# w_xo of a hybrid encoder layer as a block product of seven products, with its sums made in DRAM

## Chip, cores and metric

One core of a Trainium2 chip runs the whole layer. The metric is the time of one execution on the device in microseconds (us), the median of three runs; lower is better. The engines are TensorE (PE: matmuls; PEld: loads of the stationary operand), VectorE (DVE), ScalarE (ACT), GpSimd (POOL) and SyncE (SP, which here only issues DMAs).

## The reference

An encoder layer on x of 512 tokens by 1024 channels, all in float32: two mixers that are merged by gates, then cross-attention to a memory of 256 tokens with four heads of 256, then a SwiGLU feed-forward part of width 2816, then a final norm. The part that is changed is the end of the cross-attention:

```
q = (hn @ w_q).reshape(bsz, seq, XATTN_HEADS, XATTN_HEAD_DIM)
...
p = jax.nn.softmax(s, axis=-1).astype(v.dtype)
o = jnp.einsum('bhlm,bmhd->blhd', p, v).reshape(bsz, seq, D_MODEL)
return o @ w_o
...
h = h + memory_cross_attention(rms_norm(h, xattn_norm_g[i]), memn,
                               w_q[i], w_k[i], w_v[i], w_xo[i])
h = h + swiglu(rms_norm(h, ffn_norm_g[i]), w_gate[i], w_up[i], w_down[i])
return rms_norm(h, final_norm_g)
```

`w_o` is the kernel's `w_xo`, 1024 by 1024.

## The kernel before

**Products in two parts.** Each float32 operand is split into a high part, rounded to the format of the matmul (`hi`, a ScalarE cast), and the rest (`lo`, a VectorE subtraction): `split`, lines 83 to 86. A product is three matmuls, hi·hi, hi·lo and lo·hi (`mm3`). The sum of squares of a norm runs on ScalarE, the power -1/2 on GpSimd, the scaling on VectorE, and TensorE transposes the result to channels by tokens (`norm_feat`, `to_feat`).

**The plan of weights.** `plan` lists every weight block in the order of its use, with the function that loads it and the one that splits it. `next_w` (line 330) hands out entry i; it also issues the loads of the entries some places ahead (`LOADS` = 3, for the feed-forward jobs 4 to 7) and the splits of the next two. Raw blocks, hi and lo have three buffers each. Most blocks are 512 KB, 128 partitions by 1024.

**Block products of seven.** The weights of `w_proj_b`, `w_q`, the feed-forward jobs (`plan_unit`) and `w_down` are multiplied in blocks of two by two with seven products instead of eight (Strassen's scheme with fewer additions, numbered 1 to 7). That needs sums of weight blocks: 4, 5, 6 and 7 are made of blocks of the matrix, 1, 2 and 3 are plain blocks. For `w_proj_b`, `w_q` and `w_down` DMAs make these sums ahead in a scratch tensor in DRAM: a copy on SP's queue and an accumulating DMA on GpSimd's queue. `plan_sums` (line 257) says at which entries of the plan each pair is issued, and pins the copies in the order of the program. In a feed-forward job the sum is made in SBUF (tile `t`). The left operand needs sums of token blocks in the same way; results are added onto each other in PSUM or by VectorE.

**The order of the work.** The program gives the order of priorities and a scheduler orders each engine's instructions by its own estimate of time. `in_order` keeps an instruction at its place; `later(n, f)` puts work off by n steps; `tick` counts steps.

**Around the change.** After the products of `w_q` come, for the four heads, `scores` (softmax over 256 memory tokens; VectorE and ScalarE), `turn` (transposes of the probabilities, split into p_hi and p_lo) and `values` (line 1399: the product with V into bank `po`, split into ot_hi and ot_lo). The output product `w_xo` is a plain one: for the left 512 columns `tokm` (line 1475) with four token blocks of 128, eight row blocks of 128 and three matmuls each; its hooks `second` and `last_two` put the values of heads 1 to 3 between. The right 512 columns come next, token blocks 0 and 1, then 2 and 3 (lines 1486 to 1500). `add_evac` (line 1291) adds a result to the residual h and sums squares; `feat_norm` makes fn, the normed input of the feed-forward part, for one token block at a time. The feed-forward part starts with `gate_part(0, T0)` (line 1575) on tokens 0 to 255 and the first 512 rows, T1 are tokens 256 to 511. `idle_product` (line 1114) is one matmul whose result nobody reads, pinned at its place in TensorE's order.

PSUM has five banks of the pool `bank` and three of `aux`. The pools of the feed-forward part open where those of the attention close (`at.close()`).

Of the kernel before, what the change touches and what calls it, by code (L numbers as in the profile page):

```python
# [9 lines left out]
F32 = mybir.dt.float32  # L10
F32R = mybir.dt.float32r
# [41 lines left out]
def hybrid_layer_kernel(  # L53
# [173 lines left out]

    def plan_units(units, down):
# [25 lines left out]
    def down_sum(q, c):  # L254
        return dsum[q][:, 2 * c:min(2 * c + 2, NF // 2), :]

    def plan_sums(places):
# [10 lines left out]
        for q, i, jc, more in ((5, 0, 0, lambda c: down_block(0, 1, c)), (7, 0, 1, lambda c: down_block(1, 1, c)),  # L268
                               (6, 1, 1, lambda c: down_sum(5, c)), (4, 1, 0, lambda c: down_sum(6, c))):
            for c in range(CHUNKS):  # L270
                jobs.append((down_sum(q, c), down_block(i, jc, c), more(c)))
# [44 lines left out]
    plan_tok(w_xo, 0, KD)  # L316
    for i in range(4):
        plan_block(w_xo, 2 * i, 2, 512, 512, place=(None, None, 2, 4)[i])
# [1080 lines left out]
    def values(hd, p_hi, p_lo):  # L1399
        for dt_ in range(2):  # L1400
# [4 lines left out]
            split(ot_hi[:, 2 * hd + dt_, :], ot_lo[:, 2 * hd + dt_, :], ps)  # L1405
# [49 lines left out]
    ot_lo = slot("E", (P, KD, T), F32R, "ot_lo")  # L1455
    values(0, *pts.pop(0))
    probs2 = scores(2)
    probs3 = scores(3)
    turn(1, probs1)
# [10 lines left out]
    g_f = gain(ffn_norm_g[0], "g_f")  # L1470
    ot = (ot_hi, ot_lo)
    fn_hi, fn_lo = token_slot("fn", AWAY)
    fn = (fn_hi, fn_lo)

    tokm(w_xo, 0, ot, KD, add_evac(0, 1, None), hooks={1: second, 2: last_two})
# [6 lines left out]
    full = fp.tile([P, KD, T], F32, tag="full", name="full", bufs=1)  # L1482


    fin = add_evac(1, 1, feat_norm(g_f, fn_hi, fn_lo, full))
    held = []
    for t0 in (0, 2):
        ps = {t: bank(f"pt{t - t0}") for t in (t0, t0 + 1)}
        for wi in range(2):
            if t0 == 0:  # L1490
                held.append((wi,) + next_w(w_xo, 2 * wi, 2, 512, 512))
            for t in ps:
                tok_block(ps[t], t, held[wi:wi + 1], ot, 2, slice(0, 512), wi == 0, False)
            tick(2.7)
        if t0 == 0:
            held += [(wi,) + next_w(w_xo, 2 * wi, 2, 512, 512) for wi in (2, 3)]
        for t in ps:
            tok_block(ps[t], t, held[2:4], ot, 2, slice(0, 512), False, True)
            fin(t, ps[t])
            tick(2.7)  # L1500
# [133 lines left out]
    for i, u in enumerate(UNITS):  # L1634
# [7 lines left out]
        if i == 0:  # L1642
            split(*fn_q(K0, T1), s3)
# [165 lines left out]
```

## Time and profile before

| | |
|---|---|
| median of three runs | 892.96 us (892.39 to 893.35) |
| the profiled execution's own time | 893.12 us |
| its span, first to last instruction | 891.3 us |
| mean granted TensorE clock | 0.997 |
| TensorE busy | 881.1 us, 5744 matmuls |
| VectorE busy | 642.5 us |
| ScalarE busy | 487.4 us |
| GpSimd busy | 106.9 us |
| moved by DMA | 165.36 MB |

A page of the profile shows busy times, the span in 40 slices, DMA queues, the chain of work that ended last, and the costliest groups of instructions. L86 is line 86 of the kernel. `out<-in` names the tiles an instruction writes and reads; `pt` are the banks of w_xo, `po` those of the values. A listed matmul is longer than the distance to the next one, since matmuls overlap. In a list of waits stand the engine, what it waited to do, for whom, the sum, the times and the longest.

### The profile page before, as it was taken

What the parts mean: (1) busy time and instruction counts of PE and PEld (TensorE: products, weight loads), DVE (VectorE), ACT (ScalarE), POOL (GpSimd) and SP (SyncE); (2) the same over time, 40 slices, a digit from 0 to 9 for tenths busy, and PEclk for the clock granted to TensorE, in tenths of its full rate; (3) what the DMA queues carried; (4) which work ended last, traced back from release to release, by engine and by line L of the source; (5) the groups of instructions that cost most, each with busy time, mean ns of one, the idle gap of its engine ahead of it and who ended that gap; (6) DMA issues with size and microseconds to landing.
All of it is one profiled execution on the core that took longest, in us unless ns stands there. A gap on an engine that the chain in (4) does not pass through costs nothing.

```text
span 891.3 us, 14796 instructions
## 1 busy us (share of the span) xinstructions
PE 881.1 (99%) x5744; PEld 788.0 (88%) x5744; DVE 642.5 (72%) x1048; ACT 487.4 (55%) x714; POOL 106.9 (12%) x165
## 2 busy tenths in 40 slices
PE   9999999999999999999999999999999999999996
PEld 6788888888889998889899978999999999988875
DVE  5697653889847368658856836676878777899875
ACT  5743994244396254347656534645555455655664
POOL 1005301111032111001001001101121111000010
PEclk9999999999999999999999999999999999999998
DMA  8667456978533789834579747627899999356672
GB/s 255 196 189 182 114 155 177 189 191 190 159 87 84 212 285 268 288 117 140 168 221 256 194 103 197 166 81 181 213 237 233 216 225 249 95 167 207 204 230 102
DMA packets 118408, 165.36 MB, mean 186 GB/s; under 512 B 11825, under 2 KB 84161, under 8 KB 118210
## 3 DMA queue, kind: packets, MB, share of 16 engines
q1 hardware_dynamic: 97474, 135.74, 47.9%
q0 software_dynamic: 20576, 28.15, 19.9%
q8 instruction: 45, 0.74, 0.3%
q10 hardware_dynamic: 288, 0.52, 0.2%
q14 instruction: 25, 0.20, 0.1%
HBM read 157.61 MB, written 46.63 MB: 229 GB/s over the span
## 4 chain that ended last, share of the span: by engine, by line
PE 97%; DMA 1%; SPq 1%; ACT 0%; DVE 0%; issue 0%; POOLq 0%; ACTq 0%
PE pf L358 26%; PE pt L358 17%; PE px L1110 12%; PE dx L358 6%; PE pq L1110 6%; PE dq L358 3%; PE pv L1110 3%; PE bx L1110 3%; PE qx L1110 2%; PE dv L358 2%; PE pz L871 2%; PE pk L814 2%; PE bq L1110 1%; PE qv L1110 1%; PE psc L358 1%; PE qq L1110 1%
## 5 line engine op out<-in xcount | busy, mean ns | idle before, releaser
L86 DVE TENSOR_TENSOR wlo<-wraw,whi 128x1024 fp32r<-128x1024 f32 (+1 forms) x145 | 172.2, 1189 | 101.2 <-ACT whi L85 101.0
L85 ACT CAST whi<-wraw 128x1024 fp32r<-128x1024 f32 (+1 forms) x145 | 148.6, 1026 | 152.2 <-PE pf L358 44.0
L358 PE MATMUL pf<-xn,whi 128*128 128x512 f32 x448 | 139.6, 391 | 0.0
L358 PEld LDWEIGHTS pf<-xn,whi 128*128 128x128 f32 x448 | 83.7, 188 | 17.0
L358 PE MATMUL pf<-xn,wlo 128*128 128x512 f32 x224 | 87.3, 390 | 0.0
L1110 PE MATMUL px<-fn,whi 128*128 128x256 f32 x480 | 83.4, 277 | 0.0
L1110 PEld LDWEIGHTS px<-fn,whi 128*128 128x128 f32 x480 | 72.7, 188 | 0.2
L85 ACT CAST whi<-b 128x1024 fp32r<-128x1024 f32 x40 | 42.2, 1055 | 50.4 <-PE px L1110 27.4
L86 DVE TENSOR_TENSOR wlo<-b,whi 128x1024 fp32r<-128x1024 f32 x40 | 48.9, 1223 | 27.0 <-ACT whi L85 27.0
L1110 PE MATMUL px<-fn,wlo 128*128 128x256 f32 x240 | 66.4, 277 | 0.0
L1110 PE MATMUL pq<-s,whi 128*128 128x256 f32 x320 | 55.0, 276 | 0.0
L358 PE MATMUL dx<-whi,s 128*128 128x512 f32 x170 | 53.4, 390 | 0.4 <-DVE h L1734 0.4
L85 ACT CAST whi<-t 128x1024 fp32r<-128x1024 f32 x30 | 31.6, 1054 | 35.6 <-PE pv L1110 12.4
L86 DVE TENSOR_TENSOR wlo<-t,whi 128x1024 fp32r<-128x1024 f32 x30 | 36.7, 1225 | 19.7 <-ACT whi L85 19.7
L358 PEld LDWEIGHTS pf<-xn,wlo 128*128 128x128 f32 x224 | 42.1, 188 | 8.7
L1110 PEld LDWEIGHTS pq<-s,whi 128*128 128x128 f32 x320 | 48.3, 188 | 0.0
L1110 PEld LDWEIGHTS px<-fn,wlo 128*128 128x128 f32 x240 | 45.1, 188 | 0.0
L358 PE MATMUL pt<-whi,xn 128*128 128x512 f32 x128 | 43.7, 412 | 0.7 <-ACT xn L85 0.7
L1110 PE MATMUL pq<-s,wlo 128*128 128x256 f32 x160 | 44.2, 276 | 0.0
L358 PEld LDWEIGHTS dx<-whi,s 128*128 128x128 f32 x170 | 31.8, 188 | 7.5 <-issue 0.8
L358 PE MATMUL dx<-wlo,s 128*128 128x512 f32 x85 | 33.0, 390 | 0.0
L275 POOL DMA_DIRECT2D dsum<-in_w_down_dram x12 | 13.3, 1105 | 162.4 <-DMA dsum<-in_w_down_dram 162.4
(453 smaller groups left out, 2296.8 us busy)
## 6 DMA issues: line engine op xcount, KB each, us to landing
wraw<-in_w_in_dram SPq DMA_DIRECT2D x36, 512.0 KB, 4.7
dsum<-in_w_down_dram SPq DMA_DIRECT2D x20, 512.0 KB, 5.4
wraw<-dsum SPq DMA_DIRECT2D x20, 512.0 KB, 4.1
b<-in_w_gate_dram SPq DMA_DIRECT2D x15, 512.0 KB, 5.4
b<-in_w_up_dram SPq DMA_DIRECT2D x15, 512.0 KB, 5.3
wraw<-in_w_down_dram SPq DMA_DIRECT2D x15, 512.0 KB, 4.4
dsum<-in_w_down_dram POOLq DMA_DIRECT2D x10, 512.0 KB, 8.1
dsum<-dsum POOLq DMA_DIRECT2D x10, 512.0 KB, 8.5
```

Of the source, the lines that this page charges most:

```text
L85: hi = nc.scalar.copy(dst_hi, src)
L86: lo = nc.vector.tensor_tensor(dst_lo, src, dst_hi.bitcast(F32), ALU.subtract)
L275: plan[j + step][1].append((0, lambda d=dst, x=more: nc.gpsimd.dma_start(d, x, accum_op=ALU.add)))
L358: m = nc.tensor.matmul(ps, a[x], b[y], start=start and i == 0, stop=stop and i == 2, skip_group_check=free)
L814: nc.tensor.matmul(ps[32 * j:32 * j + 32, q, :], bd[i][:, g].rearrange("p d c -> p (d c)"), lc(es[i], g), start=(i == 0), stop=False, tile ...
L871: nc.tensor.matmul(ps[:, g, :], wt[:, g, :], u[:, o * GO + g, :], start=True, stop=True)
L1110: nc.tensor.matmul(ps[:, j, :], a[x], b[y], start=start and j == k == i == 0, stop=k == 3 and i == 2, skip_group_check=True)
```

## The change

- `w_xo` is computed as a block product of seven: blocks of 512 by 512 columns and 256 tokens, each product in two chunks of 256 rows. The order of products is in `XO`; results go to the residual by `onto`, some of them twice, with a plus or a minus. Between the products stand the values of heads 1 to 3.
- `values` copies its result to `of` in float32, and `attention_part` makes the operands of the seven products from it: for heads 0 and 1 those of products 1 and 7, for heads 2 and 3 those of 6, 5, 4, 2 and 3.
- The four sums of blocks are made in DRAM, in eight pieces, and `plan_sums` has new places for all that come after the first six. The sums of w_down come in the order 5, 6, 7, 4.
- The plan has 14 entries for `w_xo`, 512 KB each, where it had eight.
- In `plan_units` the loads of the first job are kept in the order of the program, as those of the second were.
- The norm of the feed-forward part comes for token blocks 0 and 1 after product 4, for 2 and 3 after product 3, the last.
- In the first feed-forward job a second `idle_product` stands before the split of `s3`.

```diff
+    XSRC = {1: (0, 0), 2: (1, 0), 3: (1, 1)}
+    xsum = {q: dp.tile([P, KD // 2, 512], F32, name=f"xsum{q}") for q in (4, 5, 6, 7)}
+    XO = ((1, 0), (7, 0), (1, 1), (7, 1), (6, 0), (5, 0), (6, 1), (5, 1), (4, 0), (4, 1), (2, 0), (2, 1), (3, 0), (3, 1))
+    def plan_xo():
+        for q, c in XO:
+            got, place = {}, 2 + 2 * c if q == 3 else None
+            def load(q=q, c=c, got=got):
+                got["raw"] = wp.tile([P, 2, 512], F32, tag="raw", name="wraw", bufs=3)
+                nc.sync.dma_start(got["raw"], xo_block(*XSRC[q], c) if q in XSRC else xo_sum(q, c))
+            plan.append(((w_xo, q, c), [(LOADS, load)], lambda got=got, place=place: halves(got.pop("raw"), place)))
...
-        made = [plan_unit(*u, ordered=i == 1) for i, u in enumerate(units)]
+        made = [plan_unit(*u, ordered=i < 2) for i, u in enumerate(units)]
...
+        for q, first, more in ((5, (0, 0), lambda c: xo_block(0, 1, c)), (7, (0, 1), lambda c: xo_block(1, 1, c)),
+                               (6, (1, 1), lambda c: xo_sum(5, c)), (4, (1, 0), lambda c: xo_sum(6, c))):
+            for c in range(2):
+                jobs.append((xo_sum(q, c), xo_block(*first, c), more(c)))
...
-    plan_sums([(5, 3), (7, 3), (9, 2), (13, 5), (14, 5), (16, 4)] + [(18 + 2 * i, 3) for i in range(8)] +
-              [(51 + 2 * i, 2) for i in range(4)] + [(85 + 3 * i, 3) for i in range(3)] +
-              [(95 + 2 * i, 2) for i in range(3)] + [(122 + 4 * i, 4) for i in range(16)])
+    plan_sums([(5, 3), (7, 3), (9, 2), (13, 5), (14, 5), (16, 4)] + [(i, 3) for i in (18, 20, 22, 23, 25, 26, 28, 29, 31, 32)] +
+              [(51 + 2 * i, 2) for i in range(5)] + [(i, 3) for i in (67, 74, 82, 87, 91, 95, 99)] +
+              [(118 + 18 * i // 5, 4) for i in range(19)] + [(187, 4)])
...
-            split(ot_hi[:, 2 * hd + dt_, :], ot_lo[:, 2 * hd + dt_, :], ps)
+            nc.scalar.copy(of[:, 2 * hd + dt_, :], ps)
+        attention_part(hd)
...
+    def attention_part(hd):
+        u = slice(2 * (hd % 2), 2 * (hd % 2) + 2)
+        lw = slice(u.start + 4, u.stop + 4)
+        a11, a12, a21, a22 = (of[:, k, t] for t in (T1, T0) for k in (u, lw))
+        def operand(q, src):
+            split(xops[q][0][:, u], xops[q][1][:, u], src)
+        if hd < 2:
+            operand(1, a11)
+            s3_ = np_.tile([P, 2, 256], F32, tag="ev", name="s3", bufs=2)
+            nc.vector.tensor_tensor(s3_, a11, a21, ALU.subtract)
+            operand(7, s3_)
+            return
+        nc.vector.tensor_tensor(a21, a21, a22, ALU.subtract)
+        nc.vector.tensor_tensor(a11, a21, a11, ALU.subtract)
+        operand(6, a11)
+        operand(5, a21)
+        operand(4, a22)
+        operand(2, a12)
+        nc.vector.tensor_tensor(a12, a12, a11, ALU.add)
+        later(2, lambda: operand(3, a12))
+    def xo_product(ps, q, c, start, stop, w=None, ts=(0, 1)):
+        hi, lo = w or next_w(w_xo, q, c)
+        a = xops[q]
+        for t in ts:
+            tsl = slice(t * P, (t + 1) * P)
+            for k in range(2):
+                mm3(ps[t], (a[0][:, 2 * c + k, tsl], a[1][:, 2 * c + k, tsl]), (hi[:, k, :], lo[:, k, :]),
+                    start and k == 0, stop and k == 1, True)
+        tick(1.35 * len(ts))
...
     turn(1, probs1)
-    def second():
-        values(1, *pts.pop(1))
-        turn(2, probs2)
-        turn(3, probs3)
-    def last_two():
-        for i in (2, 3):
-            values(i, *pts.pop(i))
...
-    tokm(w_xo, 0, ot, KD, add_evac(0, 1, None), hooks={1: second, 2: last_two})
+    ox = [bank("ox0"), bank("ox1")]
+    xo_product(ox, 1, 0, True, False)
+    values(1, *pts.pop(1))
+    turn(2, probs2)
+    oy = [bank("oy0"), aux("oy1")]
+    xo_product(oy, 7, 0, True, False)
+    values(2, *pts.pop(2))
+    turn(3, probs3)
+    xo_product(ox, 1, 1, False, True)
+    onto(ox, 2, 0, ALU.add)
+    values(3, *pts.pop(3))
+    xo_product(oy, 7, 1, False, True)
+    onto(oy, 0, 1, ALU.subtract)
+    oq = [bank("oq0"), bank("oq1")]
+    xo_product(ox, 6, 0, False, False)
+    xo_product(oq, 5, 0, True, False)
+    xo_product(ox, 6, 1, False, True)
+    onto(ox, 0, 1, ALU.subtract)
+    xo_product(oq, 5, 1, False, True)
     at.close()
...
+    onto(oq, 0, 1, ALU.add)
+    onto(ox, 0, 0, ALU.add)
+    for t in range(2):
+        half_done(t, 1)
+    onto(ox, 2, 1, ALU.subtract)
+    xo_product(oy, 4, 0, False, False)
+    xo_product(oy, 4, 1, False, True)
...
+    for t in range(2):
+        hs = h[:, t, HALF[0]]
+        nc.vector.tensor_tensor(hs, hs, oy[t], ALU.add)
+        half_done(t, 0)
+        to_fn(t, hss[:, 1, t, :])
+    ov = [bank("ov0"), bank("ov1")]
+    xo_product(ov, 2, 0, True, False)
+    xo_product(ov, 2, 1, False, True)
+    onto(ov, 2, 0, ALU.add)
+    for t in (2, 3):
+        half_done(t, 0)
+    ws = [next_w(w_xo, 3, c) for c in range(2)]
+    for t in range(2):
+        for c in range(2):
+            xo_product(oq, 3, c, False, c == 1, ws[c], (t,))
+        hs = h[:, 2 + t, HALF[1]]
+        nc.vector.tensor_tensor(hs, hs, oq[t], ALU.add)
+        half_done(2 + t, 1)
+        to_fn(2 + t, hss[:, 1, 2 + t, :])
...
         if i == 0:
+            idle_product(ops[1][0], fn_hi)
             split(*fn_q(K0, T1), s3)
```

More of the change, by code (lines that the diff above doesn't have):

```diff
@@ L315, in hybrid_layer_kernel @@
     plan_pair(w_q, qsum, False)
-    plan_tok(w_xo, 0, KD)
-    for i in range(4):
-        plan_block(w_xo, 2 * i, 2, 512, 512, place=(None, None, 2, 4)[i])
+    plan_xo()
     FS = 2560
@@ L1455, in hybrid_layer_kernel, with onto, half_done @@
     ot_lo = slot("E", (P, KD, T), F32R, "ot_lo")
+    of = slot("B", (P, KD, T), F32, "of")
+    ot_q = lambda ks, ts: (ot_hi[:, ks, ts], ot_lo[:, ks, ts])
+    xops = {1: ot_q(K0, T1), 2: ot_q(K1, T1), 4: ot_q(K1, T0), 7: ot_q(K0, T0), 3: ot_q(K0, T1)}
+    def attention_part(hd):
[18 more added lines that the diff above has]
+        later(2, lambda: operand(3, a12))
+    g_f = gain(ffn_norm_g[0], "g_f")
+    def xo_product(ps, q, c, start, stop, w=None, ts=(0, 1)):
[7 more added lines that the diff above has]
+        tick(1.35 * len(ts))
+    def onto(ps, t0, half, op):
+        for t in range(2):
+            hs = h[:, t0 + t, HALF[half]]
+            nc.vector.tensor_tensor(hs, hs, ps[t], op)
+    def half_done(t, half):
+        sum_sq(hss[:, 1, t, half:half + 1], h[:, t, HALF[half]])
     values(0, *pts.pop(0))
@@ L1458, in hybrid_layer_kernel @@
     probs3 = scores(3)
+    for q, nm in ((5, "kt_hi"), (6, "kt_lo")):
+        s_ = ap_.tile([P, KD, M], F32R, name=nm).rearrange("p (i k) t -> p i k t", i=2)
+        xops[q] = s_[:, 0], s_[:, 1]
     turn(1, probs1)
-    def second():
-        values(1, *pts.pop(1))
-        turn(2, probs2)
-        turn(3, probs3)
-    def last_two():
-        for i in (2, 3):
-            values(i, *pts.pop(i))
[L1470 to L1473, printed above, removed]
-    tokm(w_xo, 0, ot, KD, add_evac(0, 1, None), hooks={1: second, 2: last_two})
+    ox = [bank("ox0"), bank("ox1")]
[17 more added lines that the diff above has]
+    xo_product(oq, 5, 1, False, True)
     at.close()
@@ L1482, in hybrid_layer_kernel @@
     full = fp.tile([P, KD, T], F32, tag="full", name="full", bufs=1)
[L1485 to L1500, printed above, removed]
+    onto(oq, 0, 1, ALU.add)
[5 more added lines that the diff above has]
+    xo_product(oy, 4, 1, False, True)
+    fn_hi, fn_lo = token_slot("fn", AWAY)
+    fn = (fn_hi, fn_lo)
+    to_fn = feat_norm(g_f, fn_hi, fn_lo, full)
+    for t in range(2):
[10 more added lines that the diff above has]
+    ws = [next_w(w_xo, 3, c) for c in range(2)]
+    for t in range(2):
+        for c in range(2):
[4 more added lines that the diff above has]
+        to_fn(2 + t, hss[:, 1, 2 + t, :])
     s3 = np_.tile([P, 4, 256], F32, tag="gain", name="s3", bufs=2)
```

8 lines of the change are left out of this document (6 added, 2 removed).

## The prediction

> **What bounds the kernel now.** I read the page first: busy times, then the chain of work that ended last, then the waits of TensorE.
>
> ```profile
> span 891.3 us, 14796 instructions
> ...
> PE 881.1 (99%) x5744; PEld 788.0 (88%) x5744; DVE 642.5 (72%) x1048; ACT 487.4 (55%) x714; POOL 106.9 (12%) x165
> ...
> PE 97%; DMA 1%; SPq 1%; ACT 0%; DVE 0%; issue 0%; POOLq 0%; ACTq 0%
> ```
> ```profile
> PE pt L358 <- ACT ot_hi L85: 0.9, 2, 0.7
> ```
>
> TensorE is busy 99% and is 97% of the chain. Its waits in the stretch that is rewritten are two, together 0.9 us. So a matmul that goes there is worth its place in the stream, not its listed 390 ns, which overlaps the next one. The chain has 76 of them in one piece, then one clock of the stretch by itself:
>
> ```profile
> 536.38 17.32 PE pt L358 x76
> ```
>
> 17.32 / 76 = 0.228 us for a 512-wide matmul. Now the stretch of w_xo, in the timeline of TensorE (start, length, line, what it is, and in brackets its idle time before):
>
> ```profile
> 505.72 0.39 PE L358 MATMUL pt<-whi,ot_hi 128*128 128x512 f32 x1
> ...
> 514.84 0.50 PE L358 MATMUL pt<-whi,ot_hi 128*128 128x512 f32 x1 [0.27 <-ACT ot_hi L85]
> ...
> 524.53 0.50 PE L358 MATMUL pt<-whi,ot_hi 128*128 128x512 f32 x1 [0.68 <-ACT ot_hi L85]
> ...
> 563.58 0.40 PE L358 MATMUL pf<-fn,s 128*128 128x256 f32 x2
> ...
> 576.66 0.40 PE L1116 MATMUL idle<-fn 128*128 128x512 f32 x1
> 576.89 0.28 PE L358 MATMUL pf<-fn,s 128*128 128x256 f32 x1
> ```
>
> It runs from 505.7 to 563.6, 57.9 us. The groups of that window, by form:
>
> ```profile
> L358 PE MATMUL pt<-whi,ot_hi 128*128 128x512 f32 x48 | 19.5, 405 | 0.9 <-ACT ot_hi L85 0.9
> L358 PE MATMUL pt<-wlo,ot_hi 128*128 128x512 f32 x48 | 18.8, 391 | 0.0
> L358 PE MATMUL pt<-whi,ot_lo 128*128 128x512 f32 x48 | 15.9, 392 | 0.0
> L358 PE MATMUL pt<-s,ot_hi 128*128 128x512 f32 x32 | 10.2, 396 | 0.0
> ...
> L358 PE MATMUL po<-p_hi,vt 128*128 128x512 f32 x24 | 8.6, 398 | 0.0
> L358 PE MATMUL pt<-s,ot_lo 128*128 128x512 f32 x16 | 6.3, 391 | 0.0
> ...
> L86 DVE TENSOR_TENSOR wlo<-wraw,whi 128x1024 fp32r<-128x1024 f32 x4 | 4.9, 1225 | 7.1 <-ACT whi L85 7.1
> L358 PE MATMUL po<-p_lo,vt 128*128 128x512 f32 x12 | 4.8, 400 | 0.0
> L1294 DVE TENSOR_TENSOR h<-h,pt 128x512 f32<-128x512 f32 x7 | 4.6, 683 | 1.7 <-PE pt L358 1.7
> ...
> L85 ACT CAST ot_hi<-po 128x512 fp32r<-128x512 f32 x6 | 3.5, 588 | 13.7 <-PE po L358 13.7
> ...
> L1395 PE MATMUL ppt<-ident,prob 128*128 128x128 f32 x20 | 3.3, 272 | 0.0
> ...
> L520 PE MATMUL ptr<-ident,xs 128*128 128x128 f32 x16 | 2.2, 272 | 0.0
> ```
>
> The five pt groups are w_xo: 192 matmuls. The 36 of po are the values of heads 1 to 3. 228 x 0.228 = 52.0 us; with the two waits, 0.27 + 0.68 = 0.95, there remain 4.95 us for the 36 transposes and change-overs. VectorE (DVE) has room here, and less of it elsewhere:
>
> ```profile
> 505.70:536.40 30.70, 29.76 (x139) 23.58 (x138) 13.64 (x27) 11.24 (x24) 2.31 (x2) 1.00 0.45 104
> 536.40:553.70 17.30, 17.30 (x78) 14.12 (x78) 11.04 (x17) 8.65 (x17) 2.19 (x3) 1.00 0.86 242
> 553.70:561.00 7.30, 7.30 (x40) 6.16 (x38) 6.00 (x8) 5.01 (x8) 0.25 (x1) 1.00 0.01 3
> ...
> 688.60:707.60 19.00, 19.00 (x170) 19.00 (x170) 13.87 (x15) 9.92 (x13) 2.73 (x3) 1.00 0.96 233
> ...
> 784.30:808.70 24.40, 24.40 (x109) 20.20 (x108) 23.41 (x28) 15.15 (x19) 0.81 (x1) 1.00 0.70 203
> 808.70:838.70 30.00, 30.00 (x134) 24.84 (x133) 25.85 (x33) 18.30 (x25) 0.00 (x0) 1.00 0.65 197
> ```
>
> Each row is a stretch, its length, then the busy time of TensorE, weight loads, VectorE, ScalarE and GpSimd, the granted clock and the DMA share. VectorE works 30.7 of the first 55.3 us. In the down projection, which is already such a block product, it works 23.41 of 24.40 us and TensorE is busy throughout.
>
> **The change part by part.**
>
> *Matmuls.* Seven products, in two chunks each, of two token blocks, two row blocks and three matmuls: 7 x 2 x 12 = 168 for 192. 24 go: 24 x 0.228 = **-5.5 us**, all on the path. The second idle product is one 512-wide matmul; the one that exists runs from 576.66 to 576.89: **+0.23**. Values, scores and transposes keep their numbers.
>
> *VectorE.* Its work takes the place of what was removed, so I count it. Lengths, in its timeline:
>
> ```profile
> 500.98 1.28 DVE L86 TENSOR_TENSOR ot_lo<-po,ot_hi 128x512 fp32r<-128x512 f32 x2
> ...
> 508.80 1.27 DVE L86 TENSOR_TENSOR p_lo<-ppt,p_hi 128x512 fp32r<-128x512 f32 x2
> ...
> 537.99 2.36 DVE L86 TENSOR_TENSOR s<-wraw,s 128x1024 fp32r<-128x1024 f32 x2 [0.26 <-ACT s L85]
> 540.27 1.88 DVE L1294 TENSOR_TENSOR h<-h,pt 128x512 f32<-128x512 f32 x3
> ...
> 545.57 0.69 DVE L1294 TENSOR_TENSOR h<-h,pt 128x512 f32<-128x512 f32 x1 [1.69 <-PE pt L358]
> ...
> 549.75 1.42 DVE L512 SCALAR_TENSOR_TENSOR xs<-h,r,g_f 128x512 f32<-128x512 f32 x2 [0.75 <-POOL r L497]
> ...
> 562.59 0.69 DVE L86 TENSOR_TENSOR fn<-ptr,fn 128x512 fp32r<-128x512 f32 x1
> ```
>
> Three adds take 1.88, one 0.69: each further 512-wide operation costs 0.60. Two 1024-wide splits take 2.36 against 1.22 alone: 1.14. From 505.7 to the first feed-forward matmul VectorE then must do: the rest of the softmax to 508.80, 3.1; six p_lo, 3.6; for head 1 two splits and one difference, for heads 2 and 3 five splits and three sums each, 19 x 0.60 = 11.4; one operation more of head 0, 0.6; 12 weight splits (14 chunks less three ahead of the stretch, plus the first of w_gate), 12 x 1.14 = 13.7; 16 adds onto h (18 less those of token blocks 2 and 3 at the very end; before there were 8 in all), 9.6; for the norm of blocks 0 and 1 two scalings of 1.42 and two lower halves, 4.0. Sum **46.0 us**. TensorE's stream is 204 x 0.228 + 4.95 = **51.5 us**. So VectorE must work 89% of the stretch, between the 86% (25.85 / 30.00) and the 96% of the down projection. It fits, without much room, and only if nothing leaves VectorE idle for more than 5.5 us. ScalarE goes from 24.9 us by 12 copies and casts of 0.59 and five casts of twice the width to about 38: not the bound.
>
> *Waits that this opens*, from both sides. (i) Values of head 1 need p_lo, ready at 508.80 + 1.27 = 510.1. Before, 24 matmuls cover that; now 12 do, to 505.7 + 2.7 + 0.5 of transposes = 508.9: 1.2 us short, nothing if product 7 is put ahead, 1.8 with the extra operation of head 0. I take 1.2. The later values have one chunk, 2.7 us, in front. (ii) Products 6 and 4 write over banks that VectorE must first add to h, and product 2 takes the banks of product 6. Between the values of head 2 and product 2 TensorE has nine chunks, 24.6 us. VectorE has twelve required sums and splits, 7.2, nine weight splits, 10.3, and twelve adds, 7.2: 24.7. At least 0.1; at most 2.5, if VectorE works 91% of that time, the mean of the two down rows (27.1 us); I take 0.5, nearer the 96% row. (iii) The first feed-forward matmul needs blocks 0 and 1, both finished by product 4 at once, where before they came 5 us apart. Behind product 4 stand four chunks, 10.9, and 16 transposes at 4.95 / 36, 2.2: 13.1 us. VectorE has in that time two adds, 1.2, the norm, 4.0, three weight splits, 3.4, two adds of product 2, 1.2, and the last operand, 2.4: 12.2, in a chain that crosses ScalarE, GpSimd and TensorE. From 0 to 4.6 (second rival); I take 0.9, since it nearly fits. Together **2.6**; the 0.95 of before goes with the loop that had them.
>
> A rule of the Trainium skill speaks against waits here: by "TensorE: Matmul & The Clock Gate", section "Part 1: The HAM clock gate", about 3.4 us of idle TensorE halves its clock. By that rule the waits taken above cost no more than themselves, since each is shorter; the rows agree so far as they go, 1.00 granted with waits of 0.27 and 0.68.
>
> *Transfers.* Eight sums more, each a copy and an accumulate of 512 KB, and six loads more.
>
> ```profile
> q1 hardware_dynamic: 97474, 135.74, 47.9%
> q0 software_dynamic: 20576, 28.15, 19.9%
> ```
>
> A 512 KB transfer is 0.524 MB: 259 on the first queue in 47.9% of 891.3, 1.65 us of all engines each; 53.7 on the second, 3.30. So 8 x 4.95 + 6 x 1.65 = 49.5 us, 5.6% of the span on top of 68%. In the stretch it meets a share of 0.45, so it is hidden. In the feed-forward jobs the sums of w_down now come every 3.6 entries for 4: 1.94 a job of 19.0 us for 1.75, 0.9 us more, and 0.96 becomes 1.01. Nine jobs fall behind by 0.2 each, under 2 us, and loads are asked for four to seven entries of 2.7 us ahead. I take 0; without that cover it is 2 at the end. Two w_q sums move forward beside w_in, hidden the same way.
>
> *Loads of the first job, kept in order.* Four issues on SP's queue come behind w_xo's. What is pinned behind them, copies of w_down sums, has no reader for over 100 us. I take 0; if they made a weight late, it would cost about a transfer, 1.65 to 3.30, once.
>
> Sum: -5.5 + 0.23 + 2.6 - 0.95 = **-3.6**. The profiled execution took 893.12 (span 891.3 and 1.8 around it), 0.16 above the median of 892.96; so **889.4** against that median.
>
> **The rivals.** *All waits hidden*: -5.5 + 0.23 - 0.95 = -6.2, **886.8**. For it: the down projection has the same form and the same VectorE load without waits. Against: its operands were ready long before; these come from a softmax.
>
> *The norm takes the gain.* Before, from the add of block 0 (545.57) to the last lower half of block 1 (562.59 + 0.69) went 17.7 us. If it takes that again, behind product 4 there are only 13.1: a wait of 4.6 instead of 0.9, **893.1**, no change. Against: much of the 17.7 was slack that nobody pressed.
>
> *VectorE becomes the bound*, slower. Place: 505.7 to the feed-forward. What it must do is 46.0; with work that may come later but stands in its queue by then (two upper halves, one split, an add and a scaling of block 2) it is 46.0 + 1.2 + 1.1 + 0.6 + 1.4 = 50.3. The change loses once VectorE needs more than 57.9 - 0.23 = 57.7 for that, so once it works less than 87% of the time. At 86% it needs 58.5, +0.8; at the 73% of the feed-forward job shown (13.87 / 19.00) 68.9, +11.2, where however nothing pressed it. I price it at 82%, 61.3, nearer the stage of the same form: +3.6, **896.6**. For it: in this stretch each VectorE step waits for ScalarE's (7.1 us idle behind whi), and the softmax feeds it late. Against: those idles were free, since TensorE had other work, and the 4.3 us of later work can give way.
>
> *A wait long enough to slow the clock*: the second rival's 4.6 us in one piece, and after it matmuls at the pace of the kernel's start,
>
> ```profile
> 10.23 0.63 PE L358 MATMUL pt<-wlo,xn 128*128 128x512 f32 x1
> 10.66 1.05 PE L358 MATMUL pt<-whi,xn 128*128 128x512 f32 x2
> ```
>
> 0.43 apart for 0.228. Eight such cost 1.6, so 893.1 + 1.6 = **894.7**. This is what the skill's clock gate would make of such a wait; no wait of this length is in this stretch.
>
> **How the numbers follow.** Chances: forecast 0.52 (own range 887.6 to 891.0), all hidden 0.17, norm 0.15, VectorE 0.12, clock 0.04. A measurement of this kernel tells 0.2%, 1.8 us, from no change. Faster: 0.52 + 0.17 = 0.69; the same: 0.15; slower: 0.16. The range reaches below the second case by 0.6 for the transfers' order, and above over the norm and the clock to 895.5, which takes in the lower part of the VectorE case (from 893.0 + 0.8) and leaves out the rest: 886.2 to 895.5.
>
> **What would show it.** Right: w_xo matmuls 168; start of the feed-forward near 560, four us earlier; VectorE busy about 90% between; small waits of TensorE on p_lo, on h adds, on fn. Wrong: one wait over 3 us, or TensorE waiting for weight splits throughout (third rival); waits for DMA on w_xo or t; a later part of the kernel shifted by other than this difference; or a granted clock under 1.00.

## The result: slower, and where the time went

| kernel | median, us | range, runs |
|---|---|---|
| before | 893.2 | 892.39 to 896.89, 8 |
| after | 899.19 | 896.65 to 903.01, 8 |

The ratio is 1.0056, 95% interval 1.0037 to 1.0074: slower by 0.56%. (It is not the quotient of the two medians, which lie 6.0 us apart.) The forecast was 889.4, its range 886.2 to 895.5. The profiled execution of after took 896.65, the fastest of its eight; two further profiles, of slower executions, come with the experiments.

The page of after, its first lines and its DMA queues:

```profile
span 894.5 us, 14859 instructions
...
PE 879.2 (98%) x5721; PEld 786.7 (88%) x5721; DVE 662.0 (74%) x1078; ACT 500.0 (56%) x734; POOL 117.1 (13%) x173
...
q1 hardware_dynamic: 100258, 143.08, 49.9%
q0 software_dynamic: 22240, 32.35, 22.4%
```

TensorE works 1.9 us less than before and yet the span is 3.2 longer. So it waits more, or works slower. Its timeline of after, at the points that the prediction used (start, length, line, what, idle time before):

```profile
506.73 0.39 PE L382 MATMUL ox<-whi,ot_hi 128*128 128x512 f32 x1
...
555.39 0.39 PE L382 MATMUL oq<-s,ot_lo 128*128 128x512 f32 x1
555.62 1.03 PE L544 MATMUL ptr<-ident,xs 128*128 128x128 f32 x8
559.74 1.11 PE L544 MATMUL ptr<-ident,xs 128*128 128x128 f32 x4 [3.08 <-DVE xs L536]
562.25 0.80 PE L382 MATMUL pf<-fn,s 128*128 128x256 f32 x2 [1.40 <-ACT fn L85]
...
565.13 4.58 PE L382 MATMUL pf<-fn,s 128*128 128x256 f32 x22 [0.66 <-DVE ms L519]
...
596.06 0.39 PE L1134 MATMUL pq<-s,whi 128*128 128x256 f32 x2
```

One more row of before gives the end of the piece in which the two differ:

```profile
593.23 0.39 PE L1110 MATMUL pq<-s,whi 128*128 128x256 f32 x2
```

From these rows, and the spans, the difference by pieces:

| piece | before | after | difference | forecast |
|---|---|---|---|---|
| up to the first matmul of w_xo | 505.72 | 506.73 | +1.0 | 0 |
| from there to the first feed-forward matmul | 57.86 | 55.52 | -2.3 | -3.85 |
| from there to the first `pq` | 29.65 | 33.81 | +4.2 | +0.23 |
| from there to the end | 298.07 | 298.44 | +0.4 | 0 |
| sum | | | +3.2 | -3.6 |

w_xo itself is through at 555.6, 8 us ahead of the first feed-forward matmul of before. Then the gain is lost within some 40 us. The stretches of after (length; busy time of TensorE, weight loads, VectorE, ScalarE, GpSimd; granted clock; DMA share):

```profile
506.70:526.80 20.10, 20.10 (x100) 16.65 (x99) 17.82 (x37) 14.46 (x31) 1.14 (x1) 1.00 0.33 88
526.80:545.00 18.20, 18.20 (x81) 14.79 (x80) 18.15 (x27) 10.96 (x16) 0.00 (x0) 1.00 0.55 165
545.00:555.70 10.70, 10.70 (x49) 8.82 (x48) 9.43 (x15) 7.11 (x14) 1.45 (x2) 1.00 0.82 255
555.70:562.30 6.60, 2.11 (x14) 1.47 (x12) 5.21 (x8) 5.31 (x9) 1.85 (x2) 0.73 1.02 320
562.30:566.00 3.70, 2.95 (x11) 2.26 (x12) 3.62 (x10) 2.91 (x7) 0.56 (x1) 0.50 1.01 159
566.00:579.50 13.50, 13.50 (x108) 13.50 (x108) 7.70 (x10) 6.50 (x11) 3.57 (x3) 0.89 0.92 254
```

Two things happen behind w_xo. TensorE is busy for 2.11 of 6.60 us; this is the hole that the experiments speak of. And the granted clock falls. In before it is 1.00 up to 561.0, in the rows that stand with the prediction, and behind that:

```profile
563.60:576.70 13.10, 13.10 (x114) 13.10 (x113) 9.50 (x14) 7.16 (x13) 1.87 (x2) 1.00 0.69 207
```

In after, at 0.50, the 2.95 us of TensorE do the work of 1.5; at 0.89 the 13.5 do that of 12.0. So the clock costs an estimated 1.5 + 1.5 = 3.0 us after the first feed-forward matmul, and the wait of 0.66 is most of the rest of the 4.2.

What held the scaled rows `xs` of token block 1 for 3.08 us? VectorE's timeline in after:

```profile
554.52 0.14 DVE L520 TENSOR_SCALAR ms<-ms 128x1 f32<-128x1 f32 x1
554.59 1.21 DVE L86 TENSOR_TENSOR wlo<-b,whi 128x1024 fp32r<-128x1024 f32 x1
557.19 1.22 DVE L86 TENSOR_TENSOR s<-wraw,s 128x1024 fp32r<-128x1024 f32 x1 [1.39 <-ACT s L85]
558.34 0.68 DVE L1591 TENSOR_TENSOR h<-h,oq 128x512 f32<-128x512 f32 x1
558.93 1.41 DVE L536 SCALAR_TENSOR_TENSOR xs<-h,r,g_f 128x512 f32<-128x512 f32 x2
```

The rows stand behind a weight split of the feed-forward part, and this split waits. ScalarE's timeline shows for what:

```profile
556.11 1.05 ACT L85 CAST s<-wraw 128x1024 fp32r<-128x1024 f32 x1 [1.49 <-DMA wraw<-in_w_gate_dram]
557.69 1.05 ACT L85 CAST whi<-b 128x1024 fp32r<-128x1024 f32 x1 [0.53 <-DMA b<-in_w_gate_dram]
558.64 1.06 ACT L85 CAST fn<-ptr 128x512 fp32r<-128x512 f32 x2
```

The block of w_gate has not landed. SyncE's queue says when the two blocks of w_gate were asked for, in after and then in before:

```profile
545.82 0.37 SPq L137 DMA_DIRECT2D wraw<-in_w_gate_dram  x1
...
550.81 0.37 SPq L137 DMA_DIRECT2D wraw<-in_w_gate_dram  x1
```
```profile
535.50 0.37 SPq L137 DMA_DIRECT2D wraw<-in_w_gate_dram  x1
...
540.38 0.37 SPq L137 DMA_DIRECT2D wraw<-in_w_gate_dram  x1
```

Ten microseconds later, though w_xo ends eight earlier: fourteen blocks of w_xo go through the three `raw` buffers where eight did, and a block is asked for when a split frees a buffer (the load at 550.81 comes right behind a weight split that VectorE ran from 549.55 to 550.78). So there is a chain across engines: late buffer, late block, late cast, late split, and behind it in VectorE's queue something that needs no weight at all and that TensorE is waiting for.

### The profile page after: what moved, and what is told of

Same layout as the page of the kernel before. It is cut to its first block, busy times and chain, and to the rows that moved or that the text cites. A ratio compares the mean times of both kernels' runs of the same rounds, so it can differ in the third digit from the quotient of the medians.

```text
span 894.5 us, 14859 instructions
## 1 busy us (share of the span) xinstructions
PE 879.2 (98%) x5721; PEld 786.7 (88%) x5721; DVE 662.0 (74%) x1078; ACT 500.0 (56%) x734; POOL 117.1 (13%) x173
## 3 DMA queue, kind: packets, MB, share of 16 engines
q1 hardware_dynamic: 100258, 143.08, 49.9%
q0 software_dynamic: 22240, 32.35, 22.4%
## 4 chain that ended last, share of the span: by engine, by line
PE 90%; DMA 4%; DVE 3%; ACT 1%; SPq 1%; issue 0%; POOLq 0%; ACTq 0%; DVEq 0%
PE pf L382 25%; PE px L1134 12%; PE pt L382 10%; PE dx L382 6%; PE pq L1134 6%; PE dq L382 3%; PE pv L1134 3%; PE bx L1134 3%; PE dv L382 2%; PE pz L895 2%; PE pk L838 2%; PE qx L1134 2%; DVE wlo L86 1%; PE bq L1134 1%; PE ox L382 1%; PE po L382 1%
## 5 line engine op out<-in xcount | busy, mean ns | idle before, releaser
L86 DVE TENSOR_TENSOR wlo<-wraw,whi 128x1024 fp32r<-128x1024 f32 (+1 forms) x151 | 179.3, 1189 | 95.2 <-ACT whi L85 94.8
L85 ACT CAST whi<-wraw 128x1024 fp32r<-128x1024 f32 (+1 forms) x151 | 154.7, 1026 | 156.7 <-PE pf L382 43.9
L85 ACT CAST whi<-b 128x1024 fp32r<-128x1024 f32 x40 | 42.2, 1054 | 48.9 <-PE px L1134 25.9
L86 DVE TENSOR_TENSOR wlo<-b,whi 128x1024 fp32r<-128x1024 f32 x40 | 48.9, 1222 | 26.3 <-ACT whi L85 26.3
L1134 PEld LDWEIGHTS pq<-s,wlo 128*128 128x128 f32 x160 | 30.1, 188 | 0.0
```

The costliest lines, as they stand in the source:

```text
L85: hi = nc.scalar.copy(dst_hi, src)
L86: lo = nc.vector.tensor_tensor(dst_lo, src, dst_hi.bitcast(F32), ALU.subtract)
L1134: nc.tensor.matmul(ps[:, j, :], a[x], b[y], start=start and j == k == i == 0, stop=k == 3 and i == 2, skip_group_check=True)
```

## The experiments

Each ratio is to runs of the kernel before on the same chip at the same time. Those runs had medians from 893.3 to 895.4 us, so rows are compared by their ratios and not by their medians.

| label | median, us | range, runs | ratio, 95% interval |
|---|---|---|---|
| e1_norm_first | 898.42 | 896.42 to 900.68, 4 | 1.0053, 1.0032 to 1.0074 |
| e2_own_raw | 898.85 | 895.35 to 901.33, 6 | 1.0051, 1.0030 to 1.0071 |
| e3_fill | 899.82 | 897.63 to 901.56, 4 | 1.0067, 1.0047 to 1.0086 |
| e4_no_sums | 896.73 | 895.89 to 897.49, 6 | 1.0037, 1.0024 to 1.0049 |
| e5_both_queues | 893.95 | 891.43 to 896.77, 10 | 1.0001, 0.9986 to 1.0016 |
| e6_both_but_b11 | 893.12 | 890.35 to 896.50, 10 | 0.9988, 0.9969 to 1.0008 |
| e7_order_undone | 897.99 | 895.34 to 900.39, 10 | 1.0051, 1.0034 to 1.0069 |
| e8_parts_alone | 894.71 | 893.08 to 897.41, 10 | 1.0006, 0.9991 to 1.0022 |
| e9_both_no_sums | 891.16 | 888.90 to 895.82, 7 | 0.9964, 0.9943 to 0.9985 |
| e10_sums_early | 893.60 | 889.32 to 896.89, 12 | 0.9988, 0.9969 to 1.0006 |
| e11_early_own | 895.58 | 892.75 to 898.61, 12 | 1.0007, 0.9991 to 1.0022 |
| e12_b11_after_xs | 892.53 | 890.11 to 894.68, 12 | 0.9983, 0.9970 to 0.9996 |

### e1: the norm ahead of the splits on VectorE

```diff
+        norms.append(nc.vector.tensor_scalar(ms, ms, 1.0 / D, EPS, ALU.mult, ALU.add))
...
+            norms.append(nc.vector.scalar_tensor_tensor(dst[:, HALF[i]], ...))
...
+        if t == 0:
+            first.update({107: norms[-3], 108: norms[-1]})
+        else:
+            first.update({110: norms[-1]})
...
+        with (tc.issue_after(first[j].ins) if j in first else nullcontext()):
+            tiles.append(plan[j][2]())
```

> Three weight splits (second chunk of product 3, first and second block of w_gate) are put behind the norm's steps of token blocks 0 and 1 in VectorE's order; nothing else is changed. Theory 1 (VectorE's fixed order: the norm queues behind splits whose weights have not landed): the wait of TensorE's transposes on xs falls from 3.1 to under 1 us, the granted clock stays near 1.00 after 556, and the time falls by 4 to 8 us from the changed kernel's 899, to 891 to 895. Theory 2 (VectorE has too much work there, order or not): the wait moves to a weight split or to fn, the time stays within 2 us of 899. Theory 3 (the norm's own chain is too long for what stands behind product 4): the wait stays over 2 us.

The waits of TensorE in its trace:

```profile
PE pf L385 <- ACT fn L85: 3.5, 1, 3.5
...
PE ptr L547 <- DVE xs L539: 0.6, 1, 0.6
```

The wait for `xs` falls from 3.1 to 0.6, and one for the cast of `fn` rises from 1.4 to 3.5. ScalarE's timeline:

```profile
557.34 1.05 ACT L85 CAST s<-wraw 128x1024 fp32r<-128x1024 f32 x1 [2.02 <-DMA wraw<-in_w_gate_dram]
...
560.31 1.54 ACT L85 CAST fn<-ptr 128x512 fp32r<-128x512 f32 x3
```

The same fault one engine further on: ScalarE stands for 2.02 us at a cast whose block has not landed, and the cast of `fn` is behind it. The first feed-forward matmul starts at 561.90, 0.4 earlier than in after (0.9, counted from the first matmul of w_xo, at 507.25 here). By its outcome the run meets theory 2: the wait moved to `fn`, and 898.42 is within 2 us of 899. It can't tell theory 2 from a first theory with two queues in it, since VectorE too runs weight splits, at 558.41 and 560.15, ahead of the lower half of `fn`. The row that speaks for the queues is ScalarE's: it stood for a block and not for VectorE. e5 and e6 test it.

### e2: a buffer of its own for the second block of w_gate

```diff
-            got["raw"] = wp.tile([P, k, n], F32, tag="raw", name="wraw", bufs=3)
+            got["raw"] = np_.tile([P, k, n], F32, tag="gain", name="graw", bufs=2) if own else \
+                wp.tile([P, k, n], F32, tag="raw", name="wraw", bufs=3)
```

> The second block of w_gate is loaded into a buffer of its own instead of one of the three raw buffers, so its load need not wait for the split three entries before. Theory 1b (the split is late because the load is, and the load is late because of the raw buffers): the block lands some 5 us earlier, ScalarE's wait for it (1.5 us) and the 3.1 us wait of the transposes go, the time is 891 to 896. Theory 2 and theory 3: within 2 us of 899.

The block is asked for at 516.72, 34 us earlier than in after. VectorE has the rows of both token blocks done before w_xo ends:

```profile
551.24 2.73 DVE L537 SCALAR_TENSOR_TENSOR xs<-h,r,g_f 128x512 f32<-128x512 f32 x4
```

but on ScalarE

```profile
555.20 1.99 ACT L85 CAST whi<-b 128x1024 fp32r<-128x1024 f32 x2 [3.37 <-DMA b<-in_w_gate_dram]
...
559.61 1.53 ACT L85 CAST fn<-ptr 128x512 fp32r<-128x512 f32 x3
```

So the chain of the norm isn't too long: it can be through in time. The second rival's reason falls, though its price was right. The time stays at 898.85, not at 891 to 896: one block landing early only moves the wait to another, here `b`, a plain block of the first job, asked for at 549.14.

### e3: idle products in the hole

```diff
-            xo_product(oq, 3, c, False, c == 1, ws[c], (t,))
+            xo_product(oq, 3, c, False, c == 1, ws[c], (t,), 16 * t * c)
```

The last argument is a number of 512-wide matmuls into a spare bank.

> Sixteen 512-wide matmuls whose result nobody reads stand behind the last product of w_xo, so that TensorE is not idle while it waits for the norm. The wait itself stays. If the lowered granted clock (0.73, 0.50 and 0.89 in the three stretches from 555.7 to 579.5) comes from the wait, the clock stays at 1.00 there, and the time falls by what the half clock costs, 2 to 4 us: 895 to 897. If the clock falls for another reason, or costs nothing, the time is 899 or some more, up to the 3.6 us that the sixteen take.

```profile
555.70:562.30 6.60, 5.61 (x31) 4.52 (x29) 6.46 (x10) 3.97 (x7) 2.74 (x2) 1.00 1.10 356
562.30:566.00 3.70, 1.66 (x8) 1.56 (x8) 3.68 (x10) 3.16 (x7) 0.56 (x1) 0.67 1.19 241
```

In these stretches the clock holds through the idle products and falls behind them, since a wait for `fn`, 3.0 us, is still there. The 895 to 897 did not come. Keeping TensorE busy did not help while the norm was late, and what the clock costs by itself this run doesn't tell.

### e4: without the sums of w_xo

The jobs that make the sums are left out, and products 4 to 7 read a plain block.

```diff
-                nc.sync.dma_start(got["raw"], xo_block(*XSRC[q], c) if q in XSRC else xo_sum(q, c))
+                nc.sync.dma_start(got["raw"], xo_block(*XSRC.get(q, (0, 1)), c))
```

> The eight sums of w_xo blocks are not made in DRAM; products 4 to 7 of w_xo read plain blocks of the same size. So 16 DMAs of 512 KB are gone, and the output of the cross-attention is not the reference's. Theory 4 (the added transfers delay loads): the waits of 0.5 us on a weight split at 447 and of 0.8 at 470 go, weights before the feed-forward part land sooner, and the time falls by 3 us or more, to 896 or less. Theory 1: the waits between 440 and 500 may go, 1 to 2 us, but the wait behind w_xo stays over 2 us and the clock still falls: 897 to 899.

The stretches ahead of w_xo in after, and then in this kernel:

```profile
446.00:452.00 6.00, 5.54 (x24) 4.24 (x24) 3.63 (x4) 3.32 (x4) 0.00 (x0) 1.00 0.58 186
...
470.00:476.00 6.00, 5.17 (x46) 5.14 (x46) 4.46 (x5) 3.84 (x6) 1.16 (x1) 1.00 0.66 199
```
```profile
446.00:452.00 6.00, 6.00 (x30) 4.94 (x29) 3.09 (x3) 3.00 (x4) 0.00 (x0) 1.00 0.76 236
...
470.00:476.00 6.00, 6.00 (x55) 6.00 (x54) 3.13 (x5) 2.90 (x4) 1.21 (x1) 1.00 0.78 194
```

0.46 + 0.83 = 1.3 us of TensorE's idle time there comes from the added transfers. The hole behind w_xo stays, 3.58 for `xs` and 1.25 for `fn`. The median, 896.73, lies between the two theories' ranges, and the interval overlaps that of after. By the traces the sums are one cost of two, the smaller one.

### e5 and e6: both queues

The splits of `b11`, of the second block of w_gate, of `b21` and of the first of w_up (entries 109 to 112) come behind the cast and the lower half of `fn` of token block 1, each on its own engine. e6 leaves b11, entry 109, where it was.

```diff
+                if "on" in first and q == 0 and tsl.start == P:
+                    first.update({j: tuple(last_split) for j in (109, 110, 111, 112)})
...
+        with ExitStack() as held_back:
+            for x in first.get(j, ()):
+                held_back.enter_context(tc.issue_after(x.ins))
+            tiles.append(plan[j][2]())
```

> As the first run, and besides the splits of the first job's b11, of the second block of w_gate, of b21 and of the first block of w_up stand behind the lower half of fn of token block 1, in VectorE's order and their casts in ScalarE's. Theory 1 in its second form (both in-order queues hold norm steps behind splits whose weights have not landed; with only VectorE mended the wait moved to ScalarE's cast of fn, 3.5 us): the waits between the last product of w_xo and the feed-forward part fall from about 6.5 us to under 2, the granted clock stays at 1.00, and the time falls to 890 to 894. Theory 2 (too much work on VectorE): a wait of 3 us or more stands on the next weight split, and the time stays over 896. Theory 3 (the chain of the norm is too long): the transposes or fn are still waited for by more than 3 us with no split ahead of them.

> As the run before, but b11 of the first job keeps its place ahead of the norm of block 1, as in the changed kernel. Theory 1: if b11 lands in time, as it did (ScalarE waited 0.3 us for it), the time is that of the run before within 1 us, with less to do behind it; if b11 is late the wait of xs comes back by up to 2 us.

Both take back the 5 us: the intervals hold one. In e5 no wait between w_xo and the first feed-forward matmul is over 0.8, but one of 1.6 appears later, at the lower half of `fn` of another token block: three of the splits that were put back stand ahead of it in VectorE's queue there (567.75 to 571.3). In e6 no wait behind w_xo is over 0.97. The two show something about the clock; stretches of 2 us, first e5 and then e6:

```profile
560.00:562.00 2.00, 1.10 (x8) 0.66 (x6) 2.00 (x5) 2.00 (x4) 0.00 (x0) 1.00 1.02 340
562.00:564.00 2.00, 1.31 (x8) 1.11 (x9) 2.00 (x4) 2.00 (x3) 0.00 (x0) 1.00 0.98 326
```
```profile
556.00:558.00 2.00, 1.38 (x11) 0.90 (x9) 2.00 (x4) 1.46 (x4) 0.25 (x1) 1.00 1.00 315
558.00:560.00 2.00, 0.62 (x3) 0.41 (x3) 2.00 (x6) 2.00 (x4) 0.23 (x1) 0.93 1.07 369
560.00:562.00 2.00, 1.66 (x7) 1.66 (x8) 1.54 (x3) 1.90 (x3) 1.84 (x2) 0.50 0.41 112
...
564.00:566.00 2.00, 2.00 (x11) 2.00 (x11) 1.79 (x4) 0.00 (x0) 0.03 (x1) 0.50 1.17 273
```

In e5 TensorE is busy for 2.41 of 4 us and keeps its clock. In e6 it is busy for 2.00 of 4, with no wait over 0.97 us, and is then held at half speed for 6.8 us (559.7 to 566.5), most of them fully busy.

### e7 and e8: the other two edits of the change

e7 takes the ordered loads of the first job out of after (`ordered=i == 1`). e8 is the kernel before with the ordered loads and the second idle product, and with nothing else.

> The changed kernel with the loads of the first job free again, as they were before. Theory 1: the loads of t and b22 may go ahead of those of w_xo and w_gate and make these later, so the wait behind w_xo grows, 899 to 903. If the order of these loads were itself the cause of the late splits, the wait shrinks by 2 us or more and the time is 897 or less.

> The kernel before with two small parts of the change alone: the first job's loads in order and the second idle product. Every theory: within 1 us of the kernel before, since neither touches w_xo; the idle product is 0.23. If one of the two is what costs, 3 us or more above it.

e8 is the kernel before, 1.0006. So the two edits cost nothing that can be measured there, and the loss belongs to the rest of the change. e7 met neither condition: it is not slower than after and not faster. The hole goes elsewhere, 1.7 us of waits inside product 3 for the split of its weight and 2.2 us at the transposes. The free loads do what theory 1 said of them: a block of w_xo lands late, and ScalarE stands 3.97 us for it at 551.16.

The clock of e7 corrects what e5 and e6 seem to say. TensorE is busy for 1.76 of 4 us, less than in e6, with a wait of 2.16 us in one piece, and the clock stays:

```profile
560.50:564.50 4.00, 1.76 (x9) 1.06 (x8) 4.00 (x6) 2.75 (x6) 0.00 (x0) 1.00 0.73 250
```

### e9 to e12: do the two costs add up?

e9 is e6 with e4's edit. e10 is e6 with three of the eight sums placed earlier; e11 is e10 with e2's edit, e12 is e10 with the split of b11 (a plain block, not a sum) behind the scaled rows of token block 1 on VectorE.

```diff
-              [(51 + 2 * i, 2) for i in range(5)] + [(i, 3) for i in (67, 74, 82, 87, 91, 95, 99)] +
+              [(51 + 2 * i, 2) for i in range(8)] + [(i, 3) for i in (87, 91, 95, 99)] +
```
```diff
+        else:
+            first.update({109: norms[-1:]})
```

> The kernel of e6 without the sums of w_xo in DRAM: products 4 to 7 of w_xo read a plain block in place of a summed one, so those products multiply the wrong weights and the output is not the reference's. If the two costs are separate (added transfers ahead of w_xo, held norm behind it), both come off: e6 stood 1.16 + 0.70 = 1.9 us in the stretch 446 to 449, which vanishes, and the feed-forward starts about 1.9 us earlier than in e6 (558.8), near 557, the total near 891 (ratio 0.996 to 0.998). If the cost of the transfers is only shifted and the feed-forward's first blocks set the time in any case, the first feed-forward product stays within 0.5 us of 558.8 and the total at 893. In both the gap of 3.3 us between the last product of w_xo and the first of the feed-forward is not touched by this edit.

> The kernel of e6 with the last three of the eight sums of w_xo placed earlier, at entries 61, 63 and 65 of the plan of weights in place of 67, 74 and 82 (each with its second half two entries later). Output as the reference's. If the wait at 446 to 449 is the loads of w_v standing behind these sums in the DMA queues, it goes (0 to 0.5 us in place of 1.9), and the whole comes to 891 to 892.5, ratio about 0.997 to 0.999. If the wait comes from the amount of the transfers and not from their place, a wait of 1 to 2 us shows elsewhere ahead of 505 and the time stays at 893.

> The kernel of e10, and the second block of w_gate loaded into a buffer of its own (as in e2). Output as the reference's. If what is left of the gap behind w_xo in e6 (3.3 us) is the wait for weight blocks that a busy raw buffer holds back, the gap falls to 1.5 to 2.5 us and the clock stays above 0.9 in it, the total 1 us below that of e10 (ratio 0.995 to 0.998). If the gap is the chain of the norm itself (last h, xs, transposes, fn), it stays at 3 us, and the total within 0.5 us of e10.

> The kernel of e10, with the split of the next weight sum (b11) on VectorE put behind the scaled rows of token block 1. Output as the reference's. In e10 that split (1.22 us, at 553.65) stands ahead of the add of the last product and of the scaled rows at 555.38. If the rest of the gap is VectorE's order in front of these rows, the rows start about 1.2 us earlier, the transposes and the first feed-forward product (557.78 in e10, with w_xo ending at 554.4) start 0.8 to 1.2 us earlier, and the total is 1 us below e10's (ratio 0.996 to 0.999). If the add of the last product holds them (the product's own end and the add behind it), nothing moves by more than 0.4 us; and if the split of b11 is then late for its own product, a wait on s or wlo of 0.5 to 1.5 us shows in the first job and the time is as e10's.

e9 has the ratio 0.9964, as forecast, and its first feed-forward matmul at 557.33, 1.4 us ahead of e6's. So the two costs add up, as far as intervals that overlap (0.9943 to 0.9985, and e6's 0.9969 to 1.0008) can say. Not all of the 2.7 us between the profiled spans of e6 and e9 is the transfers: 1.4 is, and as much again comes between the first feed-forward matmul and the first `pq`, where the half clock lasts 3.41 us in place of 6.83. In e10 the stretches ahead of w_xo are full without anything being left out:

```profile
446.00:452.00 6.00, 6.00 (x28) 4.93 (x27) 3.58 (x4) 2.93 (x4) 0.00 (x0) 1.00 0.71 212
...
470.00:476.00 6.00, 6.00 (x56) 6.00 (x54) 3.75 (x4) 2.60 (x5) 1.19 (x1) 1.00 0.88 226
```

So in these two stretches it was the sums' place, not their amount. In the times it doesn't show: e10's ratio is e6's, 0.9988. Its profiled span is 889.3, 2.0 below before, but that execution, 891.04, is one of the quicker ones; its median is 2.4 above e9's, and that rest isn't explained. e11 missed: the gap behind w_xo stays at 3.4 us (556.3 to 559.7), product 3 waits for its own operand for 0.5, and the ratio, 1.0007, is no better than e10's. e12 half met its expectation: the first feed-forward matmul comes 2.5 us behind w_xo instead of 3.4,

```profile
556.16 0.50 PE L389 MATMUL pf<-fn,s 128*128 128x256 f32 x2 [0.78 <-ACT fn L85]
558.86 4.31 PE L389 MATMUL pf<-fn,s 128*128 128x256 f32 x22 [2.09 <-DVE ms L527]
```

and the wait grows at the next step, the lower halves of `fn` (the row names `ms`, which VectorE ran right behind them), so that `pq` starts where it did in e10. At 0.9983 e12 is the only one of the kernels that leave nothing out whose interval lies below one, but the intervals don't tell it from e6 and e10 at 0.9988; its gain, 0.17%, is under the 0.2% that the prediction set as its bound.

### e13 and e14: slower executions of after

> The changed kernel itself, profiled again. The profiled execution of the result (896.65) is the fastest of eight, and the median is 2.5 us above it. If the rest of the median is the same hole made longer (weight blocks of the first job landing later, TensorE waiting longer for the scaled rows and the cast of fn), this execution, if it takes 898 or more, shows the stretch from the last product of w_xo (555.4) to the idle product (579.5) longer by that much and every other stretch as before within 0.5 us. If it is waits elsewhere (ahead of w_xo at 447 and 471, or in the feed-forward jobs and the down projection), that stretch stays at 24 us and others grow.

> As the look before it, a third execution of the changed kernel: the two accounts make the same two claims of it, and an execution within 0.5 us of 896.65 tells nothing.

They took 898.30 and 899.70, with spans of 896.3 and 897.6. In e14 the waits of TensorE are

```profile
PE ptr L544 <- DVE xs L536: 3.9, 1, 3.9
PE ptr L544 <- DVE xt L607: 1.8, 1, 1.8
...
PE pt L382 <- DVE wlo L86: 1.2, 2, 0.6
...
PE pt L382 <- ACT whi L85: 1.0, 1, 1.0
```

Its span is 3.1 us longer than in the first profile. The hole, from the last matmul of w_xo to the first of the feed-forward, makes 0.7 of it (7.57 for 6.86). 1.2 is there at the first matmul of w_xo, behind waits at the kernel's start (`xt`) and for blocks of a weight (`pt`), and 1.1 comes behind the first `pq`. Neither account was right alone: the surplus of this execution is spread over several waits.

## Why the prediction was wrong

**What held.** The matmuls: from the first of w_xo to the first transposes behind it went 555.62 - 506.73 = 48.9 us; the 51.5 of the stream less 2.2 for 16 transposes is 49.3. VectorE's ledger: with later work in its queue 50.3 were forecast; the four stretches up to 562.3 show 17.82 + 18.15 + 9.43 + 5.21 = 50.6. Waits (i) and (ii): taken at 1.7 together, none came, although VectorE worked 18.15 of 18.20 us in the second stretch. The third rival, VectorE as the bound, was not it: 50.6 of 55.6 is 91%, above its point of 87%, and TensorE ran full while VectorE did. The second idle product and the ordered loads: no cost that can be measured in the kernel before (e8).

**The step that failed** is (iii), the norm, "I take 0.9, since it nearly fits". It cost 3.08 + 1.40 = 4.5 us, at the upper bound of 4.6. The sum of 12.2 us of work against 13.1 of cover counted the weight splits by their length and not by when they can start. (By that sum alone nothing would have waited; the 0.9 that was taken is a choice without a working.) What the runs showed: these splits stood waiting for blocks (1.49 us of ScalarE's time in after, 2.02 in e1, 3.37 in e2) with the norm's steps behind them, first in VectorE's queue, and in ScalarE's once that was cleared (e1). With both cleared the 5 us came back (e5, e6). A page of the Trainium skill, "TensorE: Matmul & The Clock Gate", section "Part 1: The HAM clock gate", under "Architectural detail", says that the queues of ScalarE and VectorE are strictly first in, first out; the rows agree, the cast of `fn` at 560.31 in e1 coming behind one that stood for 2.02.

The second rival had the size by luck and the wrong reason: its chain of 17.7 us wasn't the limit, since in e2 the rows were ready before w_xo ended. Two of the prediction's own signs of being wrong appeared, a wait over 3 us and a granted clock under 1.00.

**What followed from it** is the fourth rival, held at 0.04: the clock. Its 1.6 us were too few, an estimated 3.0 in after. The rule of that page of the Trainium skill, read as 3.4 us of idle time in one piece, was a poor guide to its chance: in e6 the clock fell with no wait over 0.97 us. "No wait of this length is in this stretch" looked at single waits where several short ones were enough.

**A second step that failed** is the transfers, "I take 0". The eight sums delayed weights ahead of w_xo, +1.0 in the profiled execution; e4 removes 1.3 us of idle time there and e10 does it by moving three of them. The ledger of shares over the whole span was right (73.4% by the prediction, 49.9 + 22.4 = 72.3% measured) and beside the point: what counted were two places where added transfers were issued beside a block that was due. In after a copy at 431.31 and an accumulate at 436.26 stand around the last loads of w_v, from 434.63 on, and an accumulate at 459.51 just ahead of a load at 460.38; e10 has none of them there. The second wait, 0.83 us at 470.86, is the main fault once more: ScalarE stands 4.25 us at a cast for that late block, and behind it is the copy of `qv`, which needs no weight and which TensorE waits for.

**With the failed terms put right**: -3.6, and 3.6 more for the norm, 1.0 for the transfers, 3.0 for the clock, 1.7 less for (i) and (ii), give +2.3; the spans show +3.2. The remainder is of the size of the wait of 0.66 at 565.13 and of the slow clock in the hole itself (2.11 us at 0.73, an estimated 0.6). The clock's term is an estimate from the rows; no run changed the clock alone. Why the median lies another 2.5 above the profiled execution is shown in part only (e13, e14).

## What to carry to other kernels

When a stage gets shorter, check what has to be ready at its end, and count for each in-order queue not the work in front of it but the latest arrival that any work in front of it waits for. More blocks through the same few buffers make later loads wait for more splits: the loads of the next stage came 10 us later here although the stage ended 8 us earlier. Another buffer for one block was no remedy (e2, e11). Steps that need no weight go ahead of splits in every queue that they cross; moving them in one queue only moved the wait here (e1).

## What was not expected of the hardware

That the clock falls without one long wait: in e6 2.00 us busy of 4 were too few, with no wait over 0.97. The share of idle time doesn't settle it either: in e7 1.76 of 4 were enough. What the traces do show is how long the half clock lasts, always a whole multiple of 3.41 us: 3.41 in e9 to e12, 6.83 in e1, e2, e3 and e6, 10.24 in all three profiles of after and in e4 (in e10 from 559.31 to 562.73, in after from 558.73 to 568.97). Each time it ended behind some 3.4 us in which TensorE was busy almost throughout. Fixed windows of that length would fit all of this, since the same idle time can lie within one window or across two; that was not tried, and where the limit lies is open.

And that VectorE can work 18.15 of 18.20 us on operands of the running products without TensorE waiting once.
